# Sixteen experts on one core: weights fetched as blocks of four experts, or as whole rows of one

## The chip, the cores and the metric

The kernel runs on one core of a Trainium2 chip. The metric is the device time of one execution in microseconds. A change of less than about 0.2% can't be told from none with this kernel.

## The reference, cut to what matters

The program is a small diffusion-like network over 256 tokens of width 1024: two blocks with attention, then a third block that ends in a mixture of 16 experts and a final norm. The change touches the experts alone. Everything is float32.

```python
def moe_expert_choice(h, router_w, w_gate, w_up, w_down):
    cap = CAPACITY_FACTOR * T // N_EXPERTS            # 2 * 256 // 16 = 32
    aff = jax.nn.softmax((h @ router_w).astype(jnp.float32), axis=-1)
    gate, idx = lax.top_k(jnp.swapaxes(aff, 1, 2), cap)
    xs = h[bidx, idx]
    hid = jax.nn.silu(jnp.einsum('becd,edf->becf', xs, w_gate)) * jnp.einsum('becd,edf->becf', xs, w_up)
    ye = jnp.einsum('becf,efd->becd', hid, w_down) * gate[..., None].astype(h.dtype)
    return jnp.zeros_like(h).at[bidx, idx].add(ye)
...
x = x + g_f * moe_expert_choice(h2, router_w[l], expert_w_gate[l], expert_w_up[l], expert_w_down[l])
return rmsnorm_2(x, final_norm_w)
```

`w_gate[e]` and `w_up[e]` are [1024, 2048] and `w_down[e]` is [2048, 1024], 8 MB each; the 48 matrices together are 402.65 million bytes. Each is used once, with 32 rows.

## The kernel before, in words

**The stream.** `experts` lists the expert weights as 384 units of 1 MB, each a tile of 128 partitions by 2048 floats. `fetch` (issue at L2200) loads them in this order from SyncE's queue into buffers that are used in turn: unit i goes to buffer i mod 19 once all buffers are open. They are opened bit by bit while the block before still works: four (`xw0`), then two (`xw1`), then the two raw and six split buffers of the earlier weight stream (`raw`, `wh`, `wl`), then five (`xw2`). `take(n)` first issues what has a free buffer, then hands out the next n units. A buffer is free again when the products that read it are done. After the last unit `fetch` loads the final norm's weight (`fn`).

**The order of the units.** The experts go in four quads `qd`, and the 2048 hidden columns in four blocks `f` of 512. For each (qd, f) there are eight units of gate, eight of up, eight of down. A gate or up unit is a block of 512 rows by 512 columns of one expert, in four pieces of 128 rows; so a partition gets four pieces of 2 KB. A down unit is 256 whole rows of 1024 columns; a partition gets two pieces of 4 KB. The last eight units (qd 3, f 3) are blocks of 512 by 512 of down, half after half of the columns, and the very last is loaded in four quarters.

**The products.** TensorE's array is used as four groups of 32 columns. The 32 chosen rows of an expert are the stationary operand (`xsT`, in tiles `xsA` and `xB`), the weights stream through. The four groups hold the four experts of a quad: one PSUM bank `gu` gets 4 x 32 partitions by 512 columns. `take(4)` hands out one unit of each expert, and the loop over the four row pieces k stands outside that over the experts e:

```python
for k in range(4):
    for e in range(4):
        c = (4 * qd + e) * CAP
        nc.tensor.matmul(ps[32 * e:32 * e + 32, :], lhsT=xsT[kk][:, k, c:c + CAP],
                         rhs=un[e][:, k, :], start=kk + k == 0, stop=kk == 1 and k == 3)
```

So the four units of a group are freed nearly together. ScalarE makes silu of the gate bank, VectorE multiplies by the up bank (L2404), four transposes (L2407) and a copy (L413 or L415) give `ehT`, the stationary operand of the down products (L2416), which add up in two banks `ye` over the four f. A float32 product is two instructions of TensorE in the profile.

**Gates and scatter.** `gather` picks the chosen rows with a 0/1 matrix S; its second half runs inside the first group. `gates` multiplies S by the probabilities for all 16 experts at once (POOL, L2347) and transposes the result (L2354). `scatter(qd, ...)` ends a quad: two products by the gate vector `gf` on VectorE (L2366), four products with the transposed gates (L2371, bank `sc`) that bring each expert's rows back to their tokens, four additions to x (L2372). The last scatter also starts the final norm.

Of the kernel before, what the change touches and what calls it, by code (L numbers as in the profile page):

```python
# [7 lines left out]
F32 = mybir.dt.float32  # L8
# [59 lines left out]
# modulation vectors made on VectorE: (layer, vector)  # L68
# [5 lines left out]
IDLE = "idle"       # what a step yields that has only waited: the next work in the queue may go on  # L74


class Weights:
    """Granules of weights in the order of their use: DRAM -> raw -> exact parts (hi + lo == w)."""
# [6 lines left out]
    def add(self, src, kt, n, fmt=None):  # L85
        """src: DRAM [kt * 128, n], or a list of pieces [128, ...] of it that lie one after the other,
        or a tuple of [kt * 64, n] for each half of the partitions"""
        self.items.append((src, kt, n, fmt))
# [52 lines left out]
    def get(self, lead=1):  # L141
        """the next granule; the parts of the one after it are made meanwhile"""
# [5 lines left out]
    def more(self, n=2, spare=False):  # L148
        """where a granule has had its last use: parts of those that then have room (n = 3: no other is in use)"""
# [10 lines left out]
class K:  # L160
# [11 lines left out]
    # ---------------------------------------------------------------- pools, streams  # L172
# [18 lines left out]
    def tick(self):  # L191
        """a place between products: one step of the urgent work, now and then one of the patient"""
# [23 lines left out]
    def flush(queue, name=None):  # L216
        """finish a queue up to and with name"""
# [4 lines left out]
    def later(self, gen, wait):  # L222
        """gen after some steps; wait None: not before release()"""
# [14 lines left out]
    def release(self, n):  # L238
        """held work may start; its first n steps"""
# [38 lines left out]
    # ---------------------------------------------------------------- setup  # L278
    def setup(self):
# [26 lines left out]
        # as many columns as a part of the array has  # L306
# [18 lines left out]
    def rows(self, name, parts, queue=None):  # L325
        """rows of 128 values -> columns"""
# [67 lines left out]
    def split(self, hi, lo, src, spare=False):  # L394
        """exact parts of src: hi + lo == src"""
# [9 lines left out]
    def split_scaled(self, hi, lo, src, colv):  # L405
        """exact parts of src * column"""
# [83 lines left out]
    def xs(*hl):  # L490
        """hl: (hi, lo) [128, k, tokens] of 256 tokens each, or one of all"""
# [6 lines left out]
    def gemm_T(self, out, wh, wl, m0, xh, xl, nk, n0, n):  # L498
        """weights stationary: out[128, n] = W[:, m0:m0+128]^T x^T[:, n0:n0+n]"""
# [74 lines left out]
    def ada(self, n):  # L574
        """so much of it"""
# [38 lines left out]
    def ada_half(self, h):  # L614
        """shift and scale of the first sublayer, columns 512 * h..: loads of four steps, steps, end"""
# [39 lines left out]
    def scol(self, l, v, r, g, name, pool=None):  # L655
        """g * (1 + scale) as columns"""
# [4 lines left out]
    def store_gate(self, l, v):  # L661
        """gate v of layer l (times the norm weight that goes with it) as rows in DRAM"""
# [18 lines left out]
    def load_gate(self, tile, l, v, r):  # L681
        """the same row on every partition"""
# [10 lines left out]
    def ms_of(self, src):  # L693
        """1 / rms over 1024 columns"""
# [8 lines left out]
    def mod_T(self, xn, A, B, hT, lT, n0=0, banks=None, ds=range(KD // 2)):  # L703
        """xn: two normalised token tiles; exact parts of (xn * A + B)^T into columns n0.. (A, B columns)"""
# [22 lines left out]
    def transposed(self, xn, d2):  # L727
        """columns 256 * d2.. of two token tiles, transposed, in one bank"""
# [7 lines left out]
    def open_rows(self, n):  # L736
        """room for n streams: modulated rows, transposed, and sublayer outputs"""
# [13 lines left out]
    def next_rows(self, l, va, vb, g):  # L751
        """what resid prepares of its rows: norm * g * (1 + scale) + shift, transposed, in exact parts"""
# [4 lines left out]
    def resid(self, *ty, now=False):  # L757
        """rows of each tile t += y * (mean square)^-1/2, then prepared; y already has its gate"""
# [36 lines left out]
    def gated(self, y, src, G, t, c, add=False, late=False):  # L795
        """half c of the rows: y = src * G (or (y + src) * G), and the mean square before the gate"""
# [1752 lines left out]
```

## Time and profile before

| | us |
|---|---|
| time, median of 3 runs | 2364.47 (2363.16 to 2365.2) |
| the profiled execution: span from first to last instruction | 2365.9 |
| TensorE matmul busy | 1950.9 (82%) |
| VectorE busy | 886.2 (37%) |
| ScalarE busy | 623.0 (26%) |
| GpSimd busy | 223.5 (9%) |
| HBM read over the span | 622.63 MB, 264 GB/s |

The profile gives no time of its own for the profiled execution beside the span; the span lies 1.4 us above the median and 0.7 us above the slowest of the runs. Busy shares are means over the whole program, whose parts differ much. The page's slices are 59.1 us each. A matmul's busy time counts its whole way through a pipelined array, so it overlaps with its neighbours'.

### The profile page before, as it was taken

Reading aid. Unit: us, or ns where it says so; the run is one execution under the profiler, and the core shown is the slowest. Engines: PE = TensorE matmul, PEld = TensorE weight load, DVE = VectorE, ACT = ScalarE, POOL = GpSimd, SP = SyncE. Lnnn points to the kernel's source line nnn. Section 1 sums busy time; section 2 is a strip of 40 time slices with the busy share of each in tenths; the row PEclk is TensorE's granted clock in tenths of the full one; section 3 lists DMA queues with packets and bytes.
Section 4 is the critical chain, followed back from the end, with each engine's and each line's share of the span. In section 5 each row is a group of like instructions: output and inputs, shape, how many; then the busy total and the mean of one; then the engine's idle time right before and its main releaser. Section 6 shows DMA issues by size and latency. Waiting matters only on the chain.

```text
span 2365.9 us, 26102 instructions
## 1 busy us (share of the span) xinstructions
PE 1950.9 (82%) x10728; PEld 1197.3 (51%) x10728; DVE 886.2 (37%) x1319; ACT 623.0 (26%) x966; POOL 223.5 (9%) x256
## 2 busy tenths in 40 slices
PE   7989899999998999999989985666666666676666
PEld 4765688888787779998868731111111111111111
DVE  4547546686646656655687510000000000000001
ACT  3336433231235555644565410000000000000000
POOL 1001121111113010101342000000000000000000
PEclk9999899999999999999999989888788889888888
DMA  8546326767713235554526899999999999999998
GB/s 312 158 147 214 107 95 211 256 227 224 251 55 80 73 98 179 195 178 160 159 101 213 297 356 394 395 394 395 394 395 393 392 393 393 394 394 394 395 394 316
DMA packets 297993, 625.44 MB, mean 264 GB/s; under 512 B 17384, under 2 KB 77730, under 8 KB 294802
## 3 DMA queue, kind: packets, MB, share of 16 engines
q1 hardware_dynamic: 282992, 572.70, 67.1%
q0 software_dynamic: 14480, 50.63, 6.5%
q8 instruction: 84, 1.38, 0.2%
q10 hardware_dynamic: 402, 0.45, 0.1%
q14 instruction: 35, 0.29, 0.0%
HBM read 622.63 MB, written 1.10 MB: 264 GB/s over the span
## 4 chain that ended last, share of the span: by engine, by line
DMA 28%; PE 15%; SPq 4%; DVE 1%; issue 1%; ACT 1%; POOL 0%; POOLq 0%; DVEq 0%
PE gu L2399 7%; DMA xw<-in_expert_w_down 6%; DMA xw<-in_expert_w_up 6%; DMA xw<-in_expert_w_gate 5%; SPq L2200 4%; PE ye L2416 3%; DMA wh<-in_expert_w_down 2%; DMA wl<-in_expert_w_gate 2%; DMA raw<-in_expert_w_down 1%; PE ps L485 1%; PE ps L486 1%; PE ps L487 1%; DMA wh<-in_expert_w_gate 1%; DMA wh<-in_expert_w_up 1%; DMA wl<-in_expert_w_up 1%
## 5 line engine op out<-in xcount | busy, mean ns | idle before, releaser
L403 DVE TENSOR_TENSOR wl<-raw,wh 128x2048 fp32r<-128x2048 f32 (+3 forms) x141 | 294.7, 2095 | 232.1 <-ACT wh L396 227.2
L2404 DVE TENSOR_TENSOR s<-s,gu 128x512 f32<-128x512 f32 x16 | 11.0, 688 | 864.1 <-PE gu L2399 864.1
L396 ACT CAST wh<-raw 128x2048 fp32r<-128x2048 f32 (+2 forms) x132 | 231.2, 1757 | 213.3 <-PE ps L504 103.0
L505 PE MATMUL ps<-hx,wl 128*128 128x256 f32 (+1 forms) x848 | 272.5, 321 | 5.6 <-DVE wl L403 5.5
L503 PE MATMUL ps<-hx,wh 128*128 128x256 f32 (+1 forms) x848 | 274.1, 323 | 0.1
L504 PE MATMUL ps<-lx,wh 128*128 128x256 f32 (+1 forms) x848 | 272.9, 322 | 0.9 <-DVE lx L720 0.7
L2399 PE MATMUL gu<-xw,xB 128*32 128x512 f32 x584 | 170.2, 789 | 63.3 <-DMA xw<-in_expert_w_gate 33.9
L2403 ACT ACTIVATE s<-gu 128x512 f32<-128x512 f32 x16 | 9.6, 597 | 758.1 <-PE gu L2399 758.1
L2399 PE MATMUL gu<-xw,xsA 128*32 128x512 f32 x584 | 155.1, 763 | 58.8 <-DMA xw<-in_expert_w_up 30.8
L2416 PE MATMUL ye<-xw,ehT 128*32 128x512 f32 x624 | 134.7, 689 | 53.7 <-DMA xw<-in_expert_w_down 46.2
L505 PEld LDWEIGHTS ps<-hx,wl 128*128 128x128 f32 x848 | 160.3, 189 | 19.1 <-DVE wl L403 6.5
L503 PEld LDWEIGHTS ps<-hx,wh 128*128 128x128 f32 x848 | 160.2, 189 | 14.8 <-issue 2.5
L504 PEld LDWEIGHTS ps<-lx,wh 128*128 128x128 f32 x848 | 160.2, 189 | 14.0 <-DVE lx L720 1.4
L567 DVE SCALAR_TENSOR_TENSOR acc<-av,s,acc 128x1024 f32<-128x1024 f32 x84 | 106.1, 1281 | 42.2 <-DMA av<-in_ada_w 41.4
L2399 PEld LDWEIGHTS gu<-xw,xB 128*32 128x32 f32 x584 | 33.7, 138 | 163.3 <-DMA xw<-in_expert_w_gate 59.0
L2399 PEld LDWEIGHTS gu<-xw,xsA 128*32 128x32 f32 x584 | 31.3, 132 | 155.9 <-issue 53.7
L485 PE MATMUL ps<-wh,hidh 128*128 128x512 f32 x264 | 104.4, 395 | 0.0
L487 PE MATMUL ps<-wh,hidl 128*128 128x512 f32 x264 | 103.7, 393 | 0.0
L486 PE MATMUL ps<-wl,hidh 128*128 128x512 f32 x264 | 103.5, 392 | 0.0
L2416 PEld LDWEIGHTS ye<-xw,ehT 128*32 128x32 f32 x624 | 28.6, 123 | 136.0 <-DMA xw<-in_expert_w_down 82.4
L2399 PE MATMUL gu<-wh,xB 128*32 128x512 f32 x160 | 81.4, 819 | 17.4 <-DMA wh<-in_expert_w_gate 8.7
L2377 POOL TENSOR_TENSOR xres<-xres,fn 128x512 f32<-128x512 f32 x2 | 2.5, 1260 | 971.1 <-DMA fn<-in_final_norm_w 971.1
(560 smaller groups left out, 3627.6 us busy)
## 6 DMA issues: line engine op xcount, KB each, us to landing
xw<-in_expert_w_down SPq DMA_DIRECT2D x77, 1024.0 KB, 15.5
xw<-in_expert_w_gate SPq DMA_DIRECT2D x75, 1024.0 KB, 14.4
xw<-in_expert_w_up SPq DMA_DIRECT2D x71, 1024.0 KB, 14.4
raw<-in_ffn_w SPq DMA_DIRECT2D x64, 1024.0 KB, 5.2
av<-in_ada_w POOLq DMA_DIRECT2D x80, 512.0 KB, 5.2
raw<-in_w_in SPq DMA_DIRECT2D x28, 1024.0 KB, 5.3
araw<-in_ada_w SPq DMA_DIRECT2D x24, 1024.0 KB, 4.8
wl<-in_expert_w_up SPq DMA_DIRECT2D x22, 1024.0 KB, 14.4
```

Of the source, the lines that this page charges most:

```text
L396: self.nc.scalar.copy(hi, src)
L403: self.nc.vector.tensor_sub(lo[:, n:], src[:, n:], hi[:, n:].bitcast(F32))
L485: nc.tensor.matmul(o, lhsT=a, rhs=w[0][:, j, :], start=k0 + j == 0, stop=False)
L486: nc.tensor.matmul(o, lhsT=a, rhs=w[1][:, j, :], start=False, stop=False)
L487: nc.tensor.matmul(o, lhsT=b, rhs=w[0][:, j, :], start=False, stop=k0 + j == nk - 1)
L503: nc.tensor.matmul(out, lhsT=a, rhs=xh[:, k, n0:n0 + n], start=k == 0, stop=False)
L504: nc.tensor.matmul(out, lhsT=a, rhs=xl[:, k, n0:n0 + n], start=False, stop=False)
L505: nc.tensor.matmul(out, lhsT=b, rhs=xh[:, k, n0:n0 + n], start=False, stop=k == nk - 1)
L567: nc.vector.scalar_tensor_tensor(acc[r], w, s[:, k, r:r + 1], acc[r], op0=ALU.mult, op1=ALU.add)
L2200: self.nc.sync.dma_start(t, src)
L2399: nc.tensor.matmul(ps[32 * e:32 * e + 32, :], lhsT=xsT[kk][:, k, c:c + CAP], rhs=un[e][:, k, :], start=kk + k == 0, stop=kk == 1 and k == 3)
L2416: nc.tensor.matmul(ye[c][32 * e:32 * e + 32, :], lhsT=hT[:, k if last else 2 * kk + k, 32 * e:32 * e + 32], rhs=un[e][:, k, 0:512] if last ...
```

## The change

The experts go one by one. The four column groups of the array hold four blocks of 512 of the 2048 hidden columns of one expert, all with the same 32 rows as the stationary operand. A gate or up unit is 128 whole rows of the matrix, 8 KB per partition. A down unit is 256 rows, two neighbouring rows per partition, 8 KB that lie together in DRAM; its four products go to four partition groups of the two `ye` banks, so that each bank holds four partial sums for each of the 32 rows. The transposes that make `ehT` take every second column to match. `gates(e)` makes for each expert its gates four times over, [128, 4 x 32], and `scatter` adds the four partial sums up by its product. It runs once per expert, behind the second gate unit of the next expert. The last expert's down matrix ends with four units of 512 rows by 512 columns in pieces of 2 KB, half after half of the columns, the last in four quarters. `take` hands out one unit. Buffers, queue and the number and size of the units stay; so does all before `moe`. (The diff also takes out comments.)

```diff
-        for qd in range(4):
-            for f in range(4):
-                for W in (Wg, Wu):
-                    for kk in range(2):
-                        for e in range(4):
-                            self.units.append((W[4 * qd + e][kk * 512:(kk + 1) * 512, f * 512:(f + 1) * 512], 4))
-                for kk in range(2):
-                    for e in range(4):
-                        r = f * 512 + kk * 256
-                        if qd + f == 6:
-                            self.units.append((Wd[4 * qd + e][f * 512:(f + 1) * 512, kk * 512:(kk + 1) * 512], 4))
-                        else:
-                            self.units.append((Wd[4 * qd + e][r:r + 256, :], 2))
+        for e in range(16):
+            for W in (Wg, Wu):
+                for k in range(KD):
+                    self.units.append(W[e][k * P:(k + 1) * P, :])
+            for u in range(8 if e < 15 else 4):
+                self.units.append(Wd[e][u * 256:(u + 1) * 256, :].rearrange("(p k) n -> p (k n)", k=2))
+        for c in range(2):
+            for f in (2, 3):
+                self.units.append(Wd[15][f * 512:(f + 1) * 512, c * 512:(c + 1) * 512].rearrange("(p k) n -> p k n", k=4))
...
-    def take(self, n):
+    def take(self):
         self.fetch()
-        self.used += n
-        r = self.live[:n]
-        del self.live[:n]
-        return r
+        self.used += 1
+        return self.live.pop(0)
...
-        def gates():
-            SG = self.t([P, 2, NE, CAP], "xp1", 1, pool=tp)
...
+        def gates(e):
+            SG = self.t([P, 2, 4, CAP], "SG", 1, pool=ep)
             for t in range(2):
+                nc.gpsimd.tensor_tensor(SG[:, t], S[:, t, e, :].bitcast(F32).unsqueeze(1).to_broadcast([P, 4, CAP]),
+                                        aff[:, t, e:e + 1].unsqueeze(2).to_broadcast([P, 4, CAP]), op=ALU.mult)
+            ps = self.bank()
+            for t in range(2):
+                nc.tensor.transpose(ps[:, t * P:(t + 1) * P], SG[:, t].rearrange("p a s -> p (a s)"), self.ident)
+            GT = self.t([P, 256], "GT", 1, pool=ep)
+            self.evac(GT, ps[:, :256])
             return GT
...
+        def columns(sg, n):
+            pt = self.bank("pt")
+            for i in range(4):
+                h = 256 * (i // n) if n < 4 else 0
+                nc.tensor.transpose(pt[:, i * P:(i + 1) * P], sg[:, h + i % n:h + n * P:n], self.ident)
+            hT = self.t([P, 4, P], "ehT", 2, pool=ep)
+            self.evac(hT.rearrange("p a b -> p (a b)"), pt)
+            return hT
...
+        late = None
+        for e in range(NE):
+            last = e == NE - 1
+            gu = []
+            for i in range(2):
+                ps = self.bank("gu")
...
+                for k in range(KD):
+                    w = self.take()
...
+                    for j in range(4):
+                        nc.tensor.matmul(ps[32 * j:32 * j + 32, :], lhsT=xsT[k // 4][:, k % 4, e * CAP:(e + 1) * CAP],
+                                         rhs=w[:, j * 512:(j + 1) * 512], start=k == 0, stop=k == KD - 1)
+                    if late and k == 1:
+                        scatter(*late, range(2))
+                        late = None
+                gu.append(ps)
+                if i:
+                    GT = gates(e)
+            sg = self.s5()
+            nc.scalar.activation(sg, gu[0], AF.Silu)
+            nc.vector.tensor_tensor(sg, sg, gu[1], op=ALU.mult)
+            hT = columns(sg, 2)
             ye = [self.bank("ye") for _ in range(2)]
+            for u in range(4 if last else 8):
+                w = self.take()
+                for k in range(2):
+                    for c in range(2):
+                        j = 32 * (2 * k + (c + u) % 2)
+                        nc.tensor.matmul(ye[c][j:j + 32, :], lhsT=hT[:, 2 * (u % 2) + k, 32 * (u // 2):32 * (u // 2) + 32],
+                                         rhs=w[:, k * 1024 + c * 512:k * 1024 + c * 512 + 512], start=u < 2, stop=u >= 6)
+            if not last:
+                late = e, GT, ye
+                continue
+            hT = columns(sg, 4)
+            for c in range(2):
+                for f in (2, 3):
+                    w = self.take()
+                    for k in range(4):
+                        nc.tensor.matmul(ye[c][32 * k:32 * k + 32, :], lhsT=hT[:, k, 32 * f:32 * f + 32],
+                                         rhs=w[:, k * 512:(k + 1) * 512], start=False, stop=f == 3)
+                scatter(e, GT, ye, (c,))
```

## Rows read from the trace of the kernel before

**Rows 1.** The page, the span in 40 slices of 59.1 us.

```profile
PE   7989899999998999999989985666666666676666
...
DMA  8546326767713235554526899999999999999998
GB/s 312 158 147 214 107 95 211 256 227 224 251 55 80 73 98 179 195 178 160 159 101 213 297 356 394 395 394 395 394 395 393 392 393 393 394 394 394 395 394 316
```

**Rows 2.** DMA queues from 1380 to 2340: all packets; SyncE's queue.

```profile
DMA packets 160336, 377.70 MB, mean 393 GB/s; under 512 B 5767, under 2 KB 5767, under 8 KB 160305
...
q1 hardware_dynamic: 160161, 376.73, 103.8%
```

**Rows 3.** The chain that ended last, in order: start, length, what.

```profile
1573.83 3.63 PE ye L2416 x27
1577.46 3.36 SPq L2200
1580.92 13.94 DMA xw<-in_expert_w_gate
```

**Rows 4.** GB/s in 40 slices of 1.6 us, 1637.6 to 1701.4.

```profile
GB/s 406 411 408 406 404 397 388 387 388 387 388 384 389 387 389 387 378 387 384 388 390 387 388 387 384 387 388 389 387 387 384 388 398 415 411 408 408 403 411 411
```

**Rows 5.** DMA queues from 1684 to 1687.

```profile
DMA packets 585, 1.17 MB, mean 388 GB/s; under 512 B 16, under 2 KB 16, under 8 KB 585
```

**Rows 6.** DMA queues from 1640 to 1643.

```profile
DMA packets 320, 1.23 MB, mean 410 GB/s; under 512 B 21, under 2 KB 21, under 8 KB 319
...
q1 hardware_dynamic: 319, 1.22, 102.5%
```

**Rows 7.** DMA queues from 234.2 to 235.7, loads of `ada_w`.

```profile
DMA packets 77, 0.63 MB, mean 421 GB/s; under 512 B 0, under 2 KB 0, under 8 KB 0
...
q1 hardware_dynamic: 77, 0.63, 99.9%
```

**Rows 8.** GB/s in 40 slices of 0.3 us, 1366 to 1378.

```profile
GB/s 437 423 423 382 369 382 423 437 437 423 423 382 328 246 150 68 27 14 0 0 55 0 0 0 0 0 0 0 0 0 137 55 96 205 382 423 437 437 437 396
```

**Rows 9.** Timeline of TensorE at the first products: start, length, what.

```profile
1370.37 3.64 PE L2399 MATMUL gu<-xw,xsA 128*32 128x512 f32 x32
1373.94 3.99 PE L2334 MATMUL ps<-S,xp 128*128 128x512 f32 x16
```

**Rows 10.** The end: GB/s in slices of 1 us from 2326; timeline.

```profile
GB/s 375 385 387 389 385 389 385 389 381 389 391 385 387 383 391 385 381 389 387 389 379 389 395 344 240 223 238 227 61 0 0 0 0 0 0 254 311 410 74 0
```
```profile
2351.16 4.26 PE L2416 MATMUL ye<-xw,ehT 128*32 128x512 f32 x28 [0.67 <-DMA xw<-in_expert_w_down]
...
2355.46 0.69 DVE L2366 TENSOR_TENSOR s<-gf,ye 128x512 f32<-128x512 f32 x1 [5.23 <-PE ye L2416]
```

**Rows 11.** Timeline of TensorE: two rounds of four groups; a scatter.

```profile
1659.58 1.06 PE L2399 MATMUL gu<-wl,xsA 128*32 128x512 f32 x1
...
1660.43 1.06 PE L2399 MATMUL gu<-wl,xsA 128*32 128x512 f32 x1
...
2104.00 3.70 PE L2371 MATMUL sc<-s,S 128*128 128x512 f32 x8
```

**Rows 12.** Groups by line: busy us, mean ns, idle before.

```profile
L2347 POOL TENSOR_TENSOR xp<-S,aff 128x512 f32<-128x512 f32 x2 | 2.1, 1051 | 23.5 <-PE ps L2334 23.5
L2354 PE MATMUL ps<-ct,xp 128*128 128x128 f32 x8 | 1.1, 280 | 0.0
L415 DVE COPY S<-ps 128x512 f32<-128x512 f32 x1 | 0.7, 692 | 4.3 <-PE ps L2354 4.3
...
L2407 PE MATMUL pt<-ct,s 128*128 128x128 f32 x4 | 0.7, 286 | 1.0 <-DVE s L2404 1.0
L2366 DVE TENSOR_TENSOR s<-gf,ye 128x512 f32<-128x512 f32 x2 | 1.4, 689 | 17.6 <-PE ye L2416 17.6
```

**Rows 13.** Busy time by stretch: length, engines, granted clock, DMA share, GB/s.

```profile
1375.00:2350.00 975.00, 653.49 (x3125) 144.77 (x3123) 33.07 (x48) 18.26 (x30) 3.00 (x3) 0.86 1.04 393
...
1388.00:1403.00 15.00, 11.14 (x90) 3.02 (x82) 0.69 (x1) 0.59 (x1) 0.00 (x0) 1.00 1.04 376
```

More of the change, by code (lines that the diff above doesn't have):

```diff
@@ L2195, in fetch @@
                 return
-            src, kt = self.units[i]
-            t = pl.tile([P, 2048], F32, tag=tag, name=tag).rearrange("p (k n) -> p k n", k=kt)
-            src = src.rearrange("(k p) n -> p k n", p=P)
+            src = self.units[i]
+            t = pl.tile([P, 2048], F32, tag=tag, name=tag)
+            d = t.rearrange("p (k n) -> p k n", k=src.shape[1]) if len(src.shape) > 2 else t
             if i < len(self.units) - 1:
-                self.nc.sync.dma_start(t, src)
+                self.nc.sync.dma_start(d, src)
             else:
-                for k in range(kt):
-                    self.nc.sync.dma_start(t[:, k, :], src[:, k, :])
+                for k in range(src.shape[1]):
+                    self.nc.sync.dma_start(d[:, k, :], src[:, k, :])
             self.live.append(t)
@@ L2341, in gather, with scatter @@
                     nc.vector.tensor_scalar(xsT[c][:, i, :], ps, A[:, d:d + 1], B[:, d:d + 1], op0=ALU.mult, op1=ALU.add)
-        def gates():
-            SG = self.t([P, 2, NE, CAP], "xp1", 1, pool=tp)
+        def gates(e):
+            SG = self.t([P, 2, 4, CAP], "SG", 1, pool=ep)
             for t in range(2):
-                nc.gpsimd.tensor_tensor(SG[:, t], S[:, t].bitcast(F32), aff[:, t, :].unsqueeze(2).to_broadcast([P, NE, CAP]), op=ALU.mult)
-            GT = self.t([P, 4, 256], "S", 1, pool=mp)
-            for q2 in range(2):
-                ps = self.bank()
-                for i in range(2):
-                    for t in range(2):
-                        e0 = 4 * (2 * q2 + i)
-                        nc.tensor.transpose(ps[:, i * 256 + t * P:i * 256 + (t + 1) * P],
-                                            SG[:, t, e0:e0 + 4, :].rearrange("p e s -> p (e s)"), self.ident)
-                self.evac(GT[:, 2 * q2:2 * q2 + 2, :], ps.rearrange("p (a b) -> p a b", a=2))
+                nc.gpsimd.tensor_tensor(SG[:, t], S[:, t, e, :].bitcast(F32).unsqueeze(1).to_broadcast([P, 4, CAP]),
[5 more added lines that the diff above has]
+            self.evac(GT, ps[:, :256])
             return GT
         gather(0)
-        def scatter(qd, ye, cs):
+        def scatter(e, GT, ye, cs):
             y = {}
@@ L2370, in scatter @@
                     ps = self.bank("sc")
-                    nc.tensor.matmul(ps, lhsT=GT[:, qd, t * P:(t + 1) * P], rhs=y[c], start=True, stop=True)
+                    nc.tensor.matmul(ps, lhsT=GT[:, t * P:(t + 1) * P], rhs=y[c], start=True, stop=True)
                     nc.vector.tensor_tensor(x[:, t, h], x[:, t, h], ps, op=ALU.add)
-                    if qd == 3:
+                    if e == NE - 1:
                         ms = self.sq[t, c] = self.t([P, 1], "sq", 10)
@@ L2377, in scatter @@
                             nc.gpsimd.tensor_tensor(x[:, t, h], x[:, t, h], self.fn[:, h], op=ALU.mult)
-        for qd in range(4):
-            ye = [self.bank("ye") for _ in range(2)]
-            for f in range(4):
-                gu = []
-                for i in range(2):
-                    ps = self.bank("gu")
-                    if qd + f == 0 and i == 1:
-                        GT = gates()
-                        ST.close()
-                        ep = self.pool("ep", 1, side="right")
-                        gf = ep.tile([P, 1024], F32, name="gf")
-                        self.load_gate(gf, 2, 5, 0)
-                    for kk in range(2):
-                        un = self.take(4)
-                        if qd + f + i == 0 and kk:
-                            xsT.append(self.t([P, 4, 512], "xB", 1, pool=mp))
-                            gather(1)
-                        for k in range(4):
-                            for e in range(4):
-                                c = (4 * qd + e) * CAP
-                                nc.tensor.matmul(ps[32 * e:32 * e + 32, :], lhsT=xsT[kk][:, k, c:c + CAP],
-                                                 rhs=un[e][:, k, :], start=kk + k == 0, stop=kk == 1 and k == 3)
-                    gu.append(ps)
-                sg = self.s5()
-                nc.scalar.activation(sg, gu[0], AF.Silu)
-                nc.vector.tensor_tensor(sg, sg, gu[1], op=ALU.mult)
-                pt = self.bank("pt")
-                for i in range(4):
-                    nc.tensor.transpose(pt[:, i * P:(i + 1) * P], sg[:, i * P:(i + 1) * P], self.ident)
-                hT = self.t([P, 4, P], "ehT", 2, pool=ep)
-                self.evac(hT.rearrange("p a b -> p (a b)"), pt)
-                last = qd + f == 6
-                for kk in range(2):
-                    un = self.take(4)
-                    for k in range(4 if last else 2):
-                        for c in (kk,) if last else range(2):
-                            for e in range(4):
-                                nc.tensor.matmul(ye[c][32 * e:32 * e + 32, :], lhsT=hT[:, k if last else 2 * kk + k, 32 * e:32 * e + 32],
-                                                 rhs=un[e][:, k, 0:512] if last else un[e][:, k, c * 512:(c + 1) * 512],
-                                                 start=f + kk + k == 0, stop=k == 3 if last else f == 3 and kk + k == 2)
-                    if f == 3 and (last or kk):
-                        scatter(qd, ye, (kk,) if last else range(2))
@@ new lines, in columns @@
+        def columns(sg, n):
[12 more added lines that the diff above has]
+                ps = self.bank("gu")
+                if e == 0 and i == 1:
+                    ST.close()
+                    ep = self.pool("ep", 1, side="right")
+                    gf = ep.tile([P, 1024], F32, name="gf")
+                    self.load_gate(gf, 2, 5, 0)
+                for k in range(KD):
+                    w = self.take()
+                    if e + i == 0 and k == 4:
+                        xsT.append(self.t([P, 4, 512], "xB", 1, pool=mp))
+                        gather(1)
+                    for j in range(4):
[11 more added lines that the diff above has]
+            hT = columns(sg, 2)
+            ye = [self.bank("ye") for _ in range(2)]
+            for u in range(4 if last else 8):
[16 more added lines that the diff above has]
+                scatter(e, GT, ye, (c,))
```

## The prediction

> **What bounds the kernel now.** I read the slices of the page first [rows 1]. Up to about the 24th of 40 slices the DMA engines are busy for less than all of a slice and TensorE for 0.8 to 0.9. From the 25th on the picture is flat: DMA busy at the top of its scale, 394 or 395 GB/s in nearly every slice, the other engines with time to spare. These slices are the experts (`moe`), about 1,000 of the 2,366 us. Inside them the queue view says the same without rounding: in the 960 us from 1380 to 2340 the SyncE queue moved 376.73 MB and its packets filled 103.8% of the time of 16 engines (over 100% because neighbouring packets overlap) [rows 2]. In units of 1 MB (1.048576 million bytes) that is 359.3 units, or 2.672 us for one. The chain of waits goes the same way round again and again: a transfer lands, 27 matmul instructions run in 3.63 us, SyncE issues, the next transfer takes 14 us [rows 3]. The 3.63 us are no bound: DMA goes on meanwhile at the full rate [rows 4], so what ends last is the bytes.
>
> The rate itself is the question, and it has two levels. In one 64 us stretch it runs at 404 to 411 GB/s, then at 384 to 390, then at 403 to 415 [rows 4]. The packets tell why. At 1684 there are 585 packets for 1.17 MB, 2 KB each but for 16 small ones: 388 GB/s [rows 5]. These are gate and up weights, 512 columns of a row. At 1640 there are 320 for 1.23 MB, 4 KB each (21 small ones mark ends): 410 GB/s [rows 6]. These are down weights, whole rows of 1024 columns.
>
> **The change part by part.** *Row length.* Gate and up units become 128 whole rows, 8 KB per partition. Down units pair two rows that lie one after the other, 8 KB too. Only the last four of 384 units keep 2 KB pieces. Per engine, 2 KB at 388/16 GB/s is 84.5 ns and 4 KB at 410/16 is 159.9 ns: 75.4 ns for 2 KB more, so a packet costs about 9.1 ns besides its bytes. On that line 8 KB take 159.9 + 2 x 75.4 = 310.7 ns. The trace has 8 KB rows of its own, in the first loads of `ada_w`: 77 packets in 1.5 us, none under 8 KB, 99.9% of 16 engines, so 16 x 1500 x 0.999 / 77 = 311 ns, 421 GB/s [rows 7]. Line and row agree. One unit is then 8 packets per engine, 2.491 us. I take that. It is bounded above by the 4 KB rate (2.558 us), and below by the overlap: in the stream a 4 KB packet lasts 16 x 3000 x 1.025 / 298 = 165 ns, 5 ns more than its turn, and if 8 KB rows overlap so too, a unit takes 8 x 306 ns, 2.45 us.
>
> From the two levels the stretch should have cost (16 x 2.703 + 8 x 2.558)/24 = 2.654 us a unit. It cost 2.672, 0.7% more (other queues, small gaps). I keep the 0.7%: 2.508 us. The Trainium skill ("DMA: Bandwidth & Descriptors", Specifications) puts the smallest transfer for line rate at 512 B; by that the row length would change nothing, which is rival C. Rows 5 and 6 differ by 5.7% above that size, so the measurement decides against it here.
>
> *How many units.* By 1371 all 19 buffers (4 + 2 + 2 + 6 + 5) are full and DMA stands still [rows 8]: the products start only when routing has ended, and that does not change. So 365 units follow. Before: 365 x 2.672 = 975.3 us, which fits 1375.6 to the fall of the rate near 2350 [rows 8, 10]. After: 361 x 2.508 + 4 x 2.72 = 916.3 us. Gain 59.0 us (bounds 34.9 at 4 KB speed, 79.6 with overlap and without the 0.7%).
>
> *Restart.* Before, a group of four units frees its buffers together, 3.64 us after 1370.37 (32 instructions, two for each fp32 product), and DMA moves again about 1.6 us later [rows 8, 9]. After, the first unit is free after its own 8 instructions, 3.64/4 = 0.91 us. That is 2.7 us earlier; the four units then freed hold DMA for 10 us, past the 3.99 us of the second `gather` [rows 9]. I take 2.6; bounds 0 and 2.7.
>
> *End.* Before, 28 instructions still run after 2351.16, 4.26 us, since each quarter of the last unit stands in a row behind three others [rows 10]. After, a quarter has one product left. The last quarter would land near 2353, and I take 1 us; bounds 0 and 2. What follows (scatter, norm, store) is unchanged.
>
> *More scatters, gates per expert.* 16 scatters take the place of 4. A scatter is 8 TensorE instructions, 3.70 us [rows 11]; two products and four sums on VectorE at 0.69 us [rows 12]. The twelve more are 44 us of TensorE and 50 us of VectorE. `gates` goes from one piece (2 POOL operations of 1.05 us, 8 transposes in 1.1 us) to small ones: two POOL operations and two transposes an expert, whose nearest rows are the same ones [rows 12], so at most 2.1 us of POOL and 0.3 us of TensorE for each. All of it costs nothing while an expert's bytes take longer than its TensorE work. The bytes: 24 x 2.508 = 60.2 us. TensorE: 24 units x 0.91 = 21.8, scatter 3.7, six transposes 1.0, and between up and down product 0.69 for VectorE's product of gate and up (the size of L2366) and 0.69 for the copy, 1.4 of waiting: 27.9 us. That is at full clock. At the lower one (1.2 GHz) four instructions take 0.85 us [rows 11], a unit 1.71, and the sum is 41.0 + 7.4 + 2.0 + 1.4 = 52 us. Before, the granted clock was 0.86 on the mean [rows 13]. So the cover holds at either level, by 8 us in the worse one. A stall of 3 us between up and down, or of a scatter in front of unit 3 of the next expert, is little more than one unit of 19 in hand.
>
> *SyncE.* A wait for each unit in place of groups of four. Behind it on the queue stand only later units, and with 18 of them ahead none is late.
>
> Together 59.0 + 2.6 + 1.0 = 62.6 us. The profiled execution's span is 2365.9, 1.4 above the median of the runs; the same gain from either gives 2303 as a span and 2302 as a median. I forecast 2301.
>
> **The rivals.** *A: as above*, its own range 2284 to 2318.
>
> *B: 8 KB rows stream no faster than 4 KB ones, or little faster.* For: the 8 KB stretch is 1.5 us long and comes from a load of two or three units, not from 400 MB, and its rows lie farther apart in memory than whole matrices do. Against: straight line and row give the same number. At 410 GB/s: 361 x 2.558 x 1.007 + 10.9 = 941 us, gain 34.6 + 3.6 = 38 us, 2326. The Trainium skill (the same page, "SWDGE vs HWDGE vs iDMA") prefers packets of at most 4096 B; cut so, the rows would go at this rate. Against that stand the whole 8 KB packets of rows 7.
>
> *C: the row length is not what sets the level* (it is what the other engines do, or which matrix is read). Then the stream keeps 393 GB/s, and only restart and end remain: 3.6 us, 2361, within what can be told from no change (0.2%, 4.7 us). It is also the case in which the change does not do what it says. Against: both levels come back in every round of three matrices, and gate and up, two matrices with one packet size, have one level [rows 4].
>
> *D: slower, because TensorE becomes the pace.* The point is 60 us of TensorE per expert; from there each microsecond costs 16, and from about 64 the gain is gone. It gets there if the four column groups no longer run at once: the down products now go to two PSUM banks in turn and the four groups of a gate product share one stationary slice. If down products ran only two at a time at the lower clock, 16 x 1.71 + 8 x 3.42 + 10.8 = 65.6 us, 16 x 5.4 = 86 us more, 2301 + 86 = 2387. With no overlap at all it would be over 2800. Against: four groups overlap in both kinds of product now, the down products change banks after every four without a gap, and the busier TensorE of 1388 to 1403 was granted the full clock, 1.00 [rows 13].
>
> **How the numbers follow.** A 0.75, B 0.15, C 0.05, D 0.05. The range 2284 to 2330 takes in A with both bounds and B down to 4 KB speed; C, D and a worse B lie outside. Faster by over 0.2%: A and B, 0.90; same: C, 0.05; slower: D, 0.05.
>
> **What would show it.** Right: packets of 8 KB from 1300 on, a flat rate of 418 to 424 GB/s, DMA at the top of its scale, the stream's end near 2289, a gap before the restart shorter by 2 to 3 us. B shows as a flat 405 to 412. C shows as 8 KB packets at 393. D shows as a DMA share clearly under 100% in the stream with SyncE waiting for products and TensorE without idle time. The prediction falls if the rate in the stream is not set by bytes and packets alone.

## The result, and the profile after

The changed kernel takes 2301.29 us (median; 2300.41 to 2302.78), the kernel before, on the same chip, 2364.41 (2363.16 to 2365.2). The ratio is 0.9733, 95% interval 0.9719 to 0.9746. The forecast was 2301, range 2284 to 2330: case A. The profiled execution has a span of 2301.0 us.

The page, 40 slices of 57.5 us, and its chain line, to be read against [rows 1]:

```profile
PE   7989899999998999999979987666666677666666
PEclk9999999999999999999989988777777777777777
DMA  8446235777742125555434689999999999999997
GB/s 318 149 139 212 98 122 180 263 235 225 244 136 63 58 64 174 197 197 170 152 110 146 257 332 417 420 421 421 421 421 420 421 421 421 421 421 421 421 421 322
...
DMA 38%; PE 7%; DVE 2%; ACT 1%; issue 1%; POOL 0%; SPq 0%; POOLq 0%; DVEq 0%; ACTq 0%
```

The chain line gives shares of the whole span; before, they were DMA 28%, PE 15% and SPq, SyncE's issuing, 4%. Up to the 24th slice the picture is the old one. From the 25th on the rate is flat at 417 to 421 where it was flat at 394. The queues over the stream, 1380 to 2280 (before: [rows 2]):

```profile
DMA packets 52844, 378.24 MB, mean 420 GB/s; under 512 B 5777, under 2 KB 5777, under 8 KB 7050
...
q1 hardware_dynamic: 52666, 377.23, 101.0%
```

A third of the packets carry the same bytes, and all but 7050 are now 8 KB or more (5777 of the 7050 are small ones under 512 B). 377.23 MB are 359.8 units, so a unit takes 2.502 us; it was 2.672, and 2.508 was forecast.

The restart: GB/s in slices of 0.3 us from 1366 to 1378, and TensorE's timeline there (before: [rows 8, 9]):

```profile
GB/s 27 0 0 0 0 0 0 0 0 0 0 55 0 328 109 55 191 382 410 437 410 410 382 382 355 273 328 382 355 328 355 410 410 328 382 410 410 382 382 437
```
```profile
1367.89 3.64 PE L2400 MATMUL gu<-xw,xsA 128*32 128x512 f32 x32
1371.46 0.72 PE L2328 MATMUL ps<-S,xp 128*128 128x512 f32 x2
```

Loading goes on in the slice at 1369.9, 2.0 us after the first product. Before, it was the slice at 1375.0, 4.6 us after 1370.37.

TensorE's timeline over one expert's change of stages (start, length, what, idle before and what ended it):

```profile
2205.29 1.94 PE L2400 MATMUL gu<-wh,xB 128*32 128x512 f32 x8 [0.82 <-DMA wh<-in_expert_w_up]
2207.77 1.93 PE L2400 MATMUL gu<-wl,xB 128*32 128x512 f32 x8 [0.55 <-DMA wl<-in_expert_w_up]
2209.64 0.69 PE L2345 MATMUL ps<-ct,SG 128*128 128x128 f32 x2
2212.06 1.14 PE L2376 MATMUL pt<-ct,s 128*128 128x128 f32 x4 [1.74 <-DVE s L2410]
2213.98 1.94 PE L2418 MATMUL ye<-wh,ehT 128*32 128x512 f32 x8 [0.78 <-DVE ehT L415]
...
2220.23 1.06 PE L2418 MATMUL ye<-xw,ehT 128*32 128x512 f32 x8 [1.24 <-DMA xw<-in_expert_w_down]
...
2234.21 3.70 PE L2362 MATMUL sc<-s,GT 128*128 128x512 f32 x8
```

Each unit's eight instructions take 1.06 us, or 1.94 at the lower clock, and then TensorE waits for the next unit, which lands 2.5 us after the last. Between up and down it is late for a few us and catches up before 2220. The added work stands in the groups (busy us, mean ns, idle before):

```profile
L2357 DVE TENSOR_TENSOR s<-gf,ye 128x512 f32<-128x512 f32 x32 | 20.6, 684 | 248.5 <-PE ye L2418 236.8
L2341 POOL TENSOR_TENSOR SG<-S,aff 128x128 f32<-128x128 f32 x32 | 12.1, 399 | 822.4 <-PE ps L2345 822.4
```

Both engines sat idle before it far longer than they worked.

The stretch in one row (length, busy time of PE, PEld, DVE, ACT, POOL, then the granted clock as a share of the full one, DMA share, GB/s; before: [rows 13]):

```profile
1375.00:2285.00 910.00, 623.03 (x3247) 117.10 (x3246) 84.04 (x124) 17.06 (x36) 13.02 (x33) 0.75 1.01 420
```

The chain that ended last (start, length, what), in the stream and at the end:

```profile
1463.33 19.82 DMA xw<-in_expert_w_up
...
1483.20 19.88 DMA wh<-in_expert_w_down
...
1503.15 19.82 DMA xw<-in_expert_w_gate
...
2262.62 20.36 DMA xw<-in_expert_w_down
2282.98 0.04 issue
2283.02 1.11 PE ye L2428 x8
2284.13 0.02 issue
2284.16 0.70 DVE s L2357
2284.85 0.04 issue
2284.90 3.66 PE sc L2362 x4
2288.56 1.98 PE ye L2428 x16
```

In the stream the products have left the chain and SyncE's issues take next to nothing of it [rows 3]: transfer follows transfer. The end is not as forecast. A scatter of half the columns stands in front of the last 16 instructions. The bytes, slices of 1 us from 2261 (before: [rows 10]):

```profile
GB/s 442 410 434 418 401 442 418 426 410 432 406 395 403 389 406 381 385 391 387 385 385 377 305 256 221 242 150 53 0 0 0 0 0 0 0 221 303 410 115 0
```

The rate falls in the slice at 2283, and the span ends 18 us later; before it fell in that at 2349, 17 us before the end.

**The balance.** In slices of 0.25 us, from 2281 and then, for the kernel before, from 2347, the fall begins at 2282.9 and, before, at 2349.5:

```profile
GB/s 385 385 410 360 426 360 401 320 344 295 295 287 254 270 238 262 221 221 221 221 238 213 262 254 188 213 131 66 82 82 33 16 0 0 0 0 0 0 0 0
...
GB/s 393 393 377 393 410 385 401 385 418 393 279 287 254 262 221 221 221 221 229 221 229 229 221 270 221 262 197 229 180 66 0 0 0 0 0 0 0 0 0 0
```

From the first product to the restart: 4.6 to 2.0 us, gain 2.6. From the restart to the fall: 974.5 to 913.0, gain 61.5. From the fall to the end: 16.4 to 18.1, loss 1.7. That is 62.4 us. The spans differ by 64.9; the other 2.5 lie ahead of the experts (first product at 1370.37 and 1367.89), in code that did not change: a load of `ffn_w` in the block before was issued 3.6 us earlier already, at 1003.51 instead of 1007.07. That is one execution against another; in the control below the first product came at 1362.95. The medians differ by 63.1.

### The profile page after: what moved, and what is told of

It is laid out like the page before. It is cut to its first block, busy times and chain, and to the rows that moved or that the text cites. A ratio compares the mean times of both kernels' runs of the same rounds, so it can differ in the third digit from the quotient of the medians.

```text
span 2301.0 us, 26543 instructions
## 1 busy us (share of the span) xinstructions
PE 1923.7 (84%) x10852; PEld 1171.5 (51%) x10852; DVE 938.9 (41%) x1398; ACT 622.1 (27%) x974; POOL 233.2 (10%) x286
## 5 line engine op out<-in xcount | busy, mean ns | idle before, releaser
L413 ACT COPY GT<-ps 128x256 f32<-128x256 f32 x16 | 6.0, 372 | 879.4 <-PE ps L2345 879.4
L2400 PE MATMUL gu<-xw,xB 128*32 128x512 f32 x584 | 111.5, 851 | 62.3 <-DMA xw<-in_expert_w_gate 35.9
L2418 PE MATMUL ye<-xw,ehT 128*32 128x512 f32 x592 | 101.0, 801 | 45.6 <-DMA xw<-in_expert_w_down 37.7
L2400 PE MATMUL gu<-xw,xsA 128*32 128x512 f32 x584 | 102.3, 796 | 41.1 <-DMA xw<-in_expert_w_up 29.4
L2357 DVE TENSOR_TENSOR s<-gf,ye 128x512 f32<-128x512 f32 x32 | 20.6, 684 | 248.5 <-PE ye L2418 236.8
L2341 POOL TENSOR_TENSOR SG<-S,aff 128x128 f32<-128x128 f32 x32 | 12.1, 399 | 822.4 <-PE ps L2345 822.4
L2400 PEld LDWEIGHTS gu<-xw,xB 128*32 128x32 f32 x584 | 13.7, 124 | 152.5 <-DMA xw<-in_expert_w_up 78.1
L485 PE MATMUL ps<-wh,hx 128*128 128x512 f32 (+2 forms) x208 | 81.9, 394 | 9.6 <-DVE ST L1912 8.7
L486 PE MATMUL ps<-wl,hx 128*128 128x512 f32 (+2 forms) x208 | 80.1, 385 | 2.5 <-POOL wl L402 1.9
## 6 DMA issues: line engine op xcount, KB each, us to landing
xw<-in_expert_w_down SPq DMA_DIRECT2D x77, 1024.0 KB, 19.9
xw<-in_expert_w_gate SPq DMA_DIRECT2D x75, 1024.0 KB, 19.9
xw<-in_expert_w_up SPq DMA_DIRECT2D x71, 1024.0 KB, 19.9
```

The costliest lines, as they stand in the source:

```text
L485: nc.tensor.matmul(o, lhsT=a, rhs=w[0][:, j, :], start=k0 + j == 0, stop=False)
L486: nc.tensor.matmul(o, lhsT=a, rhs=w[1][:, j, :], start=False, stop=False)
L2357: nc.vector.tensor_tensor(y[c], gf[:, c * 512:(c + 1) * 512], ye[c], op=ALU.mult)
L2400: nc.tensor.matmul(ps[32 * j:32 * j + 32, :], lhsT=xsT[k // 4][:, k % 4, e * CAP:(e + 1) * CAP], rhs=w[:, j * 512:(j + 1) * 512], start=k ...
L2418: nc.tensor.matmul(ye[c][j:j + 32, :], lhsT=hT[:, 2 * (u % 2) + k, 32 * (u // 2):32 * (u // 2) + 32], rhs=w[:, k * 1024 + c * 512:k * 1024 ...
```

## The experiments

Each is compared with the kernel before on its own chip, and, by its time, with the changed kernel.

### The control: the changed kernel once more

> The changed kernel once more, on the same chip as the three others, to compare them with: 2301.

Measured: 2301.21 us (2298.2 to 2302.81), ratio 0.974 (0.9722 to 0.9757). In its profile, from 1400 to 2260, SyncE's queue moved 361.40 MB, 2.495 us a unit, which is the measure for the runs below. Its end repeats the changed kernel's: some 18.3 us from the fall of the rate, at 2278.1, to the end.

### Is it the row length, or the order of the work?

All of the change but the long rows. Gate and up units are blocks of 512 by 512 again, taken by four; down units are two pieces of 4 KB.

```diff
-                for k in range(KD):
-                    self.units.append(W[e][k * P:(k + 1) * P, :])
+                for kk in range(2):
+                    for j in range(4):
+                        self.units.append(W[e][kk * 512:(kk + 1) * 512, j * 512:(j + 1) * 512].rearrange("(k p) n -> p k n", p=P))
...
-                self.units.append(Wd[e][u * 256:(u + 1) * 256, :].rearrange("(p k) n -> p (k n)", k=2))
+                self.units.append(Wd[e][u * 256:(u + 1) * 256, :].rearrange("(k p) n -> p k n", p=P))
...
-            hT = columns(sg, 2)
+            hT = columns(sg, 1)
```

> The changed kernel with experts one by one, but the units cut as before: gate and up in blocks of 512 rows by 512 columns (2 KB pieces, four column blocks of one expert taken together), down in 4 KB pieces. Bytes and packets set the time (theory): the stream falls back to the two levels of 388 and 410 GB/s, 2.67 us a unit, so 361 x (2.672 - 2.502) = 61 us more and 2.7 us for a restart by fours: about 2365. The order of the work sets it (rival: one expert at a time feeds DMA better): it stays at 2301 to 2304.

Measured: 2365.95 us (2364.19 to 2371.55), ratio 1.0013 (1.0004 to 1.0022). The queues from 1400 to 2260:

```profile
GB/s 387 399 396 387 399 396 387 400 395 386 401 394 387 401 393 387 401 394 387 402 393 387 402 393 387 404 391 387 403 392 387 405 390 387 405 390 387 405 389 387
DMA packets 143640, 338.53 MB, mean 394 GB/s; under 512 B 5153, under 2 KB 5153, under 8 KB 143611
```

The two levels and the old rate are back, and with them the old time, 2.2 us or 0.1% above the kernel before. New order, per-expert gates and 16 scatters together gain nothing. The gain is the row length, all but the 2.6 us of the restart, which this run, taking gate and up by fours, does not have either. Its end is like the changed kernel's: the first half's scatter, 3.75 us, stands in front of the last 16 instructions, and from the fall of the rate at 2347.2 to the end it takes 19 us, against 16.4 before the change.

### The down units alone in 4 KB pieces

```diff
-                self.units.append(Wd[e][u * 256:(u + 1) * 256, :].rearrange("(p k) n -> p (k n)", k=2))
+                self.units.append(Wd[e][u * 256:(u + 1) * 256, :].rearrange("(k p) n -> p k n", p=P))
...
-            hT = columns(sg, 2)
+            hT = columns(sg, 1)
```

> The changed kernel, only its down units in two pieces of 4 KB per partition in place of 8 KB. Theory: 121 units after the restart cost 2.558 us in place of 2.491, 8 us more: 2309, with two levels in the stream, 421 and 410 GB/s. Rival (order of the work): 2301 and one level.

Measured: 2312.28 us (2310.89 to 2313.39), ratio 0.9781 (0.9766 to 0.9795), 11 us over the changed kernel. From 1400 to 2260:

```profile
GB/s 420 410 419 421 410 421 418 413 421 415 414 421 414 417 421 412 420 419 410 420 420 412 420 417 413 422 414 417 420 412 420 421 410 420 421 411 421 418 414 421
...
q1 hardware_dynamic: 63522, 358.16, 101.6%
```

About a third of the slices fall to between 410 and 415, and the others go up to 421: the length acts unit by unit. 358.16 MB are 2.518 us a unit, 0.0225 more, 8.1 us over 361 units, as expected. The profiled executions, 2311.6 us here and 2301.0 in the changed kernel, differ by 10.6: about 1 us of it lies ahead of the first product, 8 between the restart and the fall of the rate, and 1.5 from there to the end.

### Whole rows, but freed by fours

The gate and up products take four units at a time and step through them together (and so for down), so four buffers come free at once, as before the change.

```diff
-                for k in range(KD):
-                    w = self.take()
+                for k0 in (0, 4):
+                    un = self.take(4)
...
+                    for s in range(4):
+                        for kk in range(4):
+                            j = (s + kk) % 4
+                            nc.tensor.matmul(ps[32 * j:32 * j + 32, :], lhsT=xsT[k0 // 4][:, kk, e * CAP:(e + 1) * CAP],
+                                             rhs=un[kk][:, j * 512:(j + 1) * 512], start=k0 + s == 0, stop=k0 + s == 7)
```

> The changed kernel with 8 KB rows, but units taken and freed by fours as before. Theory: only the restart loses 2.7 us, the stream keeps 421 GB/s: 2304. Rival (freeing unit by unit is what feeds DMA): back towards 2364, with a rate near 393 GB/s.

Measured: 2302.32 us (2300.32 to 2306.99), ratio 0.9736 (0.972 to 0.9752). The stream, 1400 to 2260, runs at 421 GB/s as in the changed kernel:

```profile
1400.00:2260.00 860.00, 611.98 (x3006) 151.10 (x2994) 81.15 (x118) 12.23 (x28) 10.58 (x28) 0.87 1.01 421
```

The restart, slices of 0.3 us from 1366, with the first product at 1369.98:

```profile
GB/s 382 437 410 437 300 137 82 27 27 27 0 0 0 0 0 0 0 0 0 55 0 0 0 0 0 0 0 0 0 0 0 191 27 137 191 300 410 437 437 437
```

It restarts at 1375.3, 5.3 us after that product, against 2.0 (0.9 of the difference is that the first 32 instructions took 4.56 us here, not 3.64): the mechanism of the restart is seen in the trace. Its 3 us are too few to be told from the medians.

### The rate by row length, alone

A program of loads only: units of 1 MB (the last two kinds 2 and 4 MB) from the expert matrices, with 1, 2, 4, 8, 8, 16 and 32 KB in one piece. It leaves out the whole computation and stores zeros.

```python
stream("k1", blocks(Wg, 0, 8, 256), 2048, 16)
...
stream("k8", rows(Wg, 5, 1), 2048, 16)
stream("d8", rows(Wd, 5, 2), 2048, 16)
stream("k16", rows(Wu, 5, 2), 4096, 8)
stream("k32", rows(Wg, 10, 4), 8192, 4)
```

> No products at all: expert weights are only loaded, in stretches of 40 MB with pieces of 1, 2, 4, 8 (rows of gate, then pairs of rows of down), 16 and 32 KB per partition; the output is zeros. Theory (a packet costs 9.1 ns per engine besides 37.7 ns per KB): 350, 388, 410, 422, 422, 428 and 431 GB/s. Rival 1 (the level comes from the products or the matrix): one rate in all stretches. Rival 2 (packets stop to matter above some size): 8, 16 and 32 KB alike at 421.

Measured, span 747.6 us; the queues from 20 to 110 (1 KB), 132 to 220 (2 KB), 245 to 320 (4 KB), 350 to 420 (8 KB), 560 to 625 (16 KB) and 660 to 700 us (32 KB):

```profile
DMA packets 31079, 31.34 MB, mean 348 GB/s; under 512 B 480, under 2 KB 31079, under 8 KB 31079
...
DMA packets 17139, 34.05 MB, mean 387 GB/s; under 512 B 518, under 2 KB 518, under 8 KB 17138
...
DMA packets 7965, 30.73 MB, mean 410 GB/s; under 512 B 464, under 2 KB 464, under 8 KB 7965
...
DMA packets 4059, 29.58 MB, mean 423 GB/s; under 512 B 448, under 2 KB 448, under 8 KB 448
...
DMA packets 1928, 27.95 MB, mean 430 GB/s; under 512 B 222, under 2 KB 222, under 8 KB 222
...
DMA packets 592, 17.30 MB, mean 433 GB/s; under 512 B 64, under 2 KB 64, under 8 KB 64
```

The other 8 KB stretch, pairs of down rows, has 422. Per engine a packet of 1, 2, 4, 8, 16, 32 KB takes 47, 85, 160, 310, 610 and 1211 ns (its bytes over a sixteenth of the rate). Each doubling adds 37.5 to 37.6 ns per KB, and 9 to 10 ns are left at nought: the line drawn from two levels holds from 1 to 32 KB, with no computation beside it.

### TensorE's work doubled

Nearly every expert product is issued a second time with zeros as the stationary operand, which adds zero to the sums.

```diff
+                    for j in range(4) if e + i and k else ():
+                        nc.tensor.matmul(ps[32 * j:32 * j + 32, :], lhsT=zero, rhs=w[:, j * 512:(j + 1) * 512], start=False, stop=False)
```

> The changed kernel with nearly every gate, up and down product issued a second time, with zeros as the stationary operand, so that the sums stay as they are. TensorE's work per expert goes from 28 to 50 us at full clock and from 52 to 93 us at the lower one. Theory (bytes set the pace, 60 us per expert; TensorE is covered): no change, 2301 to 2305, if the busier TensorE is granted the full clock. Rival (TensorE is close to the pace at the clock it is granted): at the 0.75 of the changed kernel's stream some 67 us per expert, 16 x 7 = 110 us more, 2410.

Measured: 2301.52 us (2300.9 to 2302.41), ratio 0.9739 (0.9724 to 0.9753). From 1400 to 2260, this run and then the control:

```profile
1400.00:2260.00 860.00, 687.84 (x5396) 176.88 (x5384) 79.92 (x118) 12.24 (x28) 10.58 (x28) 0.98 1.01 420
...
1400.00:2260.00 860.00, 576.50 (x2981) 105.92 (x2980) 76.55 (x113) 12.23 (x28) 10.58 (x28) 0.75 1.01 421
```

Almost twice the matmuls cost nothing: TensorE is covered with room, and rival D is far off. The granted clock, 0.75 in the control, is 0.98 here. So the engine's busy time grew far less than its instructions. The time and the rate of the stream are the same at both clocks: the lower one costs the stream nothing.

### Five buffers fewer

```diff
-NX = 4, 2, 5
+NX = 4, 2, 0
```

> The changed kernel with 14 buffers in place of 19 (the last five are not opened). Theory: buffers matter only at the start, where DMA stands still until products free one: five more units after the restart, 5 x 2.5 = 12.5 us, 2314, with the same 421 GB/s in the stream. Rival (depth of the stream matters): the rate falls too, 2325 or more. Rival (start does not matter): 2301.

Measured: 2313.26 us (2312.02 to 2315.34), ratio 0.9789 (0.9774 to 0.9805). GB/s in slices of 1 us, 1340 to 1380, and the queues from 1400 to 2260:

```profile
GB/s 434 426 426 418 434 434 279 262 410 360 393 401 123 57 8 0 0 0 0 0 0 0 0 0 0 0 0 0 82 180 393 410 254 401 385 418 426 418 414 410
...
DMA packets 49630, 361.67 MB, mean 421 GB/s; under 512 B 5506, under 2 KB 5506, under 8 KB 5506
```

The DMA stands still from 1355 to 1368 (in the changed kernel's trace from 1366 to 1369), since five units less fit before the products start; 5 x 2.5 = 12.5 us, and 12.0 were lost. The stream itself keeps 421 GB/s with 14 buffers. The buffers are worth what they hold at the start and nothing after.

### Longer rows still

Since 16 KB packets are faster, five buffers become 2 MB and take two neighbouring rows of gate or up (four of down); eight stay at 1 MB, so 18 MB are held in place of 19. The chosen rows must then be gathered in pairs, and the scale columns A and B are wanted in the same order.

```diff
-NX = 4, 2, 5
+NX = 2, 1, 2
...
+        sizes = [2, 2, 2] + [1] * 8 + [2, 2]
...
+        ps = self.bank()
+        nc.tensor.transpose(ps[:16, :P], ab.rearrange("p a d -> p (a d)"), self.ident)
```

> A version meant to be faster: the same stream in 13 buffers, five of 2 MB and eight of 1 MB, with 16 KB rows (two neighbouring rows of gate or up, four of down) in the large ones and 8 KB pieces at 16 KB distance in the small ones; chosen rows are gathered in the matching order. Theory: ten eighteenths of the bytes go at 430 GB/s in place of 421, 361 x 0.026 = 9 us less; one unit less on chip at the restart and a first buffer of two units cost 3 us: 2295. Rival: packets above 8 KB bring nothing inside the kernel: 2304.

Measured: 2307.02 us (2306.35 to 2307.44), ratio 0.9762 (0.9747 to 0.9776): 6 us slower than the changed kernel, not 6 faster. The stream did what was expected, 364.36 MB on SyncE's queue from 1400 to 2260, 2.475 us a unit, 7 us less over 361 units. But the first products began at 1376.87, 9 us later than the changed kernel's 1367.89. Counted from each execution's own `ffn_w` load in the block before (1002.42 here, 1003.51 there, 999.75 in the control) they are 10 us later than in the changed kernel and 11 us later than in the control. TensorE's timeline in the block before, and the first products:

```profile
1327.50 0.38 PE L2246 MATMUL ps<-ct,s 128*16 128x128 f32 x1 [6.33 <-DVE s L2244]
1328.25 0.61 PE L2252 MATMUL ps<-ct,s 16*64 16x16 f32 x8 [0.37 <-DVE s L2248]
1328.79 0.80 PE L485 MATMUL ps<-wh,hx 128*128 128x512 f32 x1
1329.38 0.63 PE L486 MATMUL ps<-wl,hx 128*128 128x512 f32 x1
...
1376.87 3.64 PE L2434 MATMUL gu<-xw,xsA 128*32 128x512 f32 x32
```

L2246 is the transpose that I had added for A and B. In TensorE's order it waits for VectorE's copy, 6.33 us of idle time, and the products behind it run for some us at a lower rate, 0.63 us each where 0.40 is usual there: from 1320 to 1340 the granted clock is 0.74, and in the control, where TensorE has no idle time in that stretch, 1.00.

The same kernel with that transpose moved into the selection of the experts' rows, where TensorE has nothing to do, and with ScalarE's copies:

```diff
             nc.tensor.transpose(aT[0:NE, t * P:(t + 1) * P], aff[:, t, :], self.ident)
+        ps = self.bank()
+        nc.tensor.transpose(ps[:16, :P], self.ab2.rearrange("p a d -> p (a d)"), self.ident)
+        T = tp.tile([16, P], F32, name="abT")
+        nc.scalar.activation(T, ps[:16, :P], AF.Copy)
```

> The mixed 16 KB kernel (2307.0 us) streamed at 424 GB/s as forecast but its products began at 1376.87 us, 9 us later than the changed kernel's. Theory: that was the added transpose for the rearranged scale columns in block 2: TensorE waited 6.3 us behind VectorE's split of a weight, the clock of the matmuls after it fell, and the loads queued behind them. Here the same columns are transposed during the selection, where TensorE is idle, with ScalarE's copies. Theory: products begin within 1.5 us of the changed kernel's (relative to its earlier stages), 2296 to 2299 us, 2 to 5 below the changed kernel (2301.3). Rival (the 2 MB units crowd the loads of block 2): products still begin 8 to 9 us late, 2306 to 2308 us.

Measured: 2298.05 us (2292.68 to 2299.68), ratio 0.9716 (0.9703 to 0.9729). TensorE at that place:

```profile
1355.15 0.42 PE L2313 MATMUL ps<-ct,rb 128*16 128x128 f32 x1
1355.99 0.61 PE L2319 MATMUL ps<-ct,abT 16*64 16x16 f32 x8 [0.41 <-ACT abT L2315]
...
1368.60 1.93 PE L2433 MATMUL gu<-xw,xsA 128*32 128x512 f32 x16
```

The products begin at 1368.60. Against the control, which was 4.6 us ahead in the block before (its `ffn_w` load at 999.75, here 1004.33) and began at 1362.95, that is 1.1 us late. The stream moved 364.44 MB in the same stretch. So the late start came from the transpose and its copies where they stood, not from the 2 MB units. The median is the lowest of all, but 3 us, 0.14%, can't be told from the changed kernel: the intervals of the two ratios overlap.

## Why the prediction was right

*The bound.* Right: the experts go at the pace of bytes and packets. Doubled products cost nothing, short rows alone bring back the old time, and the chain after is transfer on transfer.

*The packet cost, 9.1 ns and 37.7 ns per KB.* Right, and it holds from 1 to 32 KB. The line's own limit is 16 x 1024 B in 37.6 ns, 436 GB/s. The Trainium skill ("DMA: Bandwidth & Descriptors", Where 436 GB/s comes from) gives the ports of SBUF 435 GB/s in all; the 433 measured with 32 KB agrees.

*The unit, 2.508 us.* 2.502 was measured. The line's 2.491 was right and the 0.7% for gaps a little much: 0.4%. That is 2 of the 2.5 us that the stream gave over the forecast (61.5 against 59.0). The range given for case A does not follow from its terms: their bounds add up to 2280 and 2330, not to 2284 and 2318.

*The restart, 2.6 us.* Measured 2.6, and freeing by fours gave it back (5.3 us after the first product).

*The end, gain 1.0 us.* Wrong, by size and sign: 1.7 lost, outside its bounds of 0 and 2. The step that failed is that after the last byte only one product would be left. In the new order two units come behind the first half of the last columns, where four did; at the forecast's 2.72 us each that is 5.4 us of transfer. The last unit of the first half landed at 2282.98, and its products, VectorE's product and that half's scatter, four instructions at the lower clock in 3.66 us, took until 2288.56. So the products of both last units, 16 instructions, stood behind the scatter (before, the first half's products were done at 2346.7, ahead of the fall at 2349.5, and the last products waited for a transfer [rows 10]). The short rows in the new order show the same, so the loss belongs to the order and not to the long rows. Part of it may be the clock: in both 16 KB kernels, whose transfers differ too, this scatter ran at the full clock, 1.96 us, and 17.4 us passed from the fall to the end. The order at the end alone was not tried. That more transfers under way at once (below) also made the first half land late is argued and not shown.

*Scatters, gates, waits of SyncE at no cost.* Right. POOL's two operations for an expert took 0.40 us each, under the bound of 1.05. But the 18 units that were to be ahead on the queue are about eight (below); 421 GB/s went on all the same.

*The rivals.* B (410 GB/s) fell with the flat 421: 8 KB rows kept their rate over the 377 MB of the stream. The packets stayed whole: of 52844 only 7050 are under 8 KB. The 4096 B that the prediction names from the Trainium skill ("DMA: Bandwidth & Descriptors", SWDGE vs HWDGE vs iDMA) stand there in a table of what GpSimd builds; these loads are issued by SyncE. C (row length not the cause) fell twice, by the short rows in the new order and by the loads alone. The Trainium skill's 512 B for line rate ("DMA: Bandwidth & Descriptors", Specifications) is not what these runs show: 348 GB/s with 1 KB, 433 with 32 KB. D fell with the doubled products. The sum, 62.6 us, met 62.4 in the traces, with +2.5 in the stream and -2.7 at the end; that these cancel is luck of 2 us, not of 60. The sum gave 2302 as a median; no reason stands for the 2301 that was forecast, and that it lies 0.3 us from the measured median is luck too.

## What to carry to other kernels

Where a stretch runs at full DMA share, read packets and bytes in two places with different rates: two points give the cost of a packet and of a KB, and the line foretells a layout that the kernel doesn't have yet. Then the question is only whether the work fits behind the faster stream, at the lower clock too. A small operation added in front of others in an engine's order can cost more than the gain it serves (7 us of bytes against some 10 us of late start); put it where that engine waits anyway.

## What was not expected of the hardware

*Eight transfers in flight.* In the changed kernel SyncE's next issue waits for a landing, not for a buffer:

```profile
SPq L2196 <- DMA xw<-in_expert_w_gate: 144.7, 69, 2.3
SPq L2196 <- DMA xw<-in_expert_w_up: 142.4, 68, 2.1
```

A transfer takes 19.9 us from issue to landing, and one lands every 2.5 us, so eight are under way; before, with 14 to 17 us and 2.67, five to six and a half. It costs nothing, since 421 GB/s go on. The number follows the length of the pieces: in the loads alone, with 16 buffers and no products, a unit of 1 MB took 11.9, 14.4, 18.5 and 19.9 us with pieces of 1, 2, 4 and 8 KB, at the rates above about 4, 5, 7 and 8 units under way. With 14 buffers in the kernel it took 19.9 us too. Why the number follows the pieces was not tried.

*The clock.* TensorE, busy for 0.68 of the stream (623.03 of 910 us; before 0.67 [rows 13]), was granted 0.75 of its clock on the mean, and before 0.86. With the products doubled, nearly half of them on zeros, it was busy for 0.80 and granted 0.98. Taken by fours, the same units at the same 421 GB/s gave 0.71 busy and 0.87 granted. So at nearly the same busy share work in bunches of 32 instructions was granted more of the clock than work in bunches of 8 with a short wait behind each; why, no run here shows. In the stream the lower clock is hidden behind the bytes; at the end it is not, in the 3.66 us of the scatter.
